# A section that ends without its own drain of GpSimd: bias and softmax over 571 MB on one core

## The chip, the cores and the metric

One core of one Trainium2 chip. The metric is the device time of one execution in microseconds (us); a kernel is run several times and the median is given. A profile is one execution, so its span can differ by a few us from the median.

## The reference

```python
B, H, S = (2, 8, 2112)          # logits: B x H x S x S, float32; rel_bias: H x 33
rel_clipped = np.clip(pos[:, None] - pos[None, :], -16, 16) + 16
logits = logits + rel_bias[:, rel_clipped][None]
logits = logits - logits.max(axis=-1, keepdims=True)
exp = np.exp(logits)
return exp / exp.sum(axis=-1, keepdims=True)
```

Each row of 2112 logits gets a bias that depends on the distance from the diagonal, and a softmax. 285 MB are read and 285 MB written.

## The kernel before

The 128 partitions hold 6 rows each, 50,688 bytes, in one of four buffers; 44 such loads and stores make the whole. GpSimd issues the loads (but half of the first one), SyncE issues the stores. VectorE adds the bias (a strip made once), ScalarE takes the exponential with the row sum, VectorE inverts and multiplies. The four engines' parts are written by hand, with semaphores, inside one critical section. These are the parts that matter here:

```python
    section = ctx.enter_context(tc.tile_critical(name="rows"))        # L74
    ...
    def take(eng, sem, v):
        eng.wait_ge(sem, v).then_inc(sem, -v)                           # L88
    def load(eng, u, start):
        eng.dma_start(out=L[u][:], in_=rows(logits, start)).then_inc(loaded[u], 16)   # L91
    def reload(eng, u, start):
        take(eng, stored[u], 16)          # the buffer's store has landed
        load(eng, u, start)
    ...
    def sync_part(eng):
        ...                               # 44 stores (L97), then:
        for n in range(BUFS):
            take(eng, stored[n], 32 if n < 2 else 16)   # all of them have landed

    def gpsimd_part(eng):
        row_load(eng, 1, loaded[0])       # half of the first buffer
        ...                               # loads 1 to 3
        passes(eng, BUFS, lambda u, start, loads: reload(eng, u, start))   # 40 loads
        eng.drain()                       # L246, the part's own drain
    ...
    with _tile.TileContext(nc) as tc:     # L291: the program's start and end
```

At the end of a critical section each engine that took part runs a drain (an instruction that ends when all of the engine's earlier work is done) and signals SyncE. The program then ends with two more rounds in which all engines meet, with further drains. (A NOP only waits for a signal and gives one.)

The softmax here doesn't subtract the row's maximum and nothing guards it: scores larger than these inputs give would overflow.

Of the kernel before, what the change touches and what calls it, by code (L numbers as in the profile page):

```python
# [14 lines left out]
def kernel(  # L15
# [55 lines left out]
            tensor=t.tensor, offset=t.offset + start * S, ap=[[T * S, P], [1, run]]  # L71
        )

    section = ctx.enter_context(tc.tile_critical(name="rows"))  # L74
    loaded = [nc.alloc_semaphore(f"loaded{u}") for u in range(BUFS)]
    stored = [nc.alloc_semaphore(f"stored{u}") for u in range(BUFS)]
    table = nc.alloc_semaphore("table")
# [218 lines left out]
```

## Time and profile before

| | |
|---|---|
| time, median of the first three runs | 1329.33 us (1326.05 to 1329.79) |
| span in the profile | 1324.4 us |
| VectorE, ScalarE, GpSimd busy | 71%, 40%, 3% |
| DMA | 431 GB/s over the span, busy in every slice |
| last store landed, to the last instruction's end | 1323.276 to 1324.411 us: 1.135 us |

The table is read from the bottom: the stream of transfers fills the time until SyncE sees its last store land, and what the ending adds after that is 1.1 us.

### The profile page before, as it was taken

To read this page: it belongs to the slowest core of one execution; us is meant where nothing else is said; L and a number is where in the kernel's file an instruction comes from. 1 tells how busy PE (TensorE), PEld (TensorE's weight loads), DVE (VectorE), ACT (ScalarE), POOL (GpSimd) and SP (SyncE) were. 2 spreads that over 40 slices of the span, in tenths; PEclk is the share of its full clock that TensorE was granted. 3 is DMA by queue.
4 is the path that set the end of the run, shared out by engine and by line. 5 is a ranking of instruction groups with operands and counts; after the bars stand their busy time and mean duration, and the time that the engine had idled before them with its cause. 6 is when DMAs were issued, how large, how long until landed. Compare 5 with 4: busy or idle time off the path is not lost. (4 is left out here: it accounts for less than half of the span.)

```text
span 1324.4 us, 2004 instructions
## 1 busy us (share of the span) xinstructions
DVE 941.6 (71%) x451; ACT 524.9 (40%) x530; POOL 39.8 (3%) x50
## 2 busy tenths in 40 slices
DVE  4989776677777767667777767667777776766891
ACT  0645533333444443333344443333344443333360
POOL 0000000000000000000000000000000000000000
DMA  9999999999999999999999999999999999999998
GB/s 392 438 424 437 436 433 429 439 435 427 436 435 435 430 438 435 430 433 436 435 429 439 435 429 435 438 433 430 438 435 429 435 438 433 430 438 435 432 431 371
DMA packets 13762, 570.99 MB, mean 431 GB/s; under 512 B 1600, under 2 KB 1600, under 8 KB 1600
## 3 DMA queue, kind: packets, MB, share of 16 engines
q1 hardware_dynamic: 7024, 288.72, 50.4%
q0 software_dynamic: 6592, 282.23, 49.3%
q10 hardware_dynamic: 144, 0.02, 0.0%
q14 instruction: 2, 0.02, 0.0%
HBM read 285.49 MB, written 285.47 MB: 431 GB/s over the span
## 5 line engine op out<-in xcount | busy, mean ns | idle before, releaser
L125 ACT ACTIVATE L<-L 128x2112 f32<-128x2112 f32 x264 | 515.2, 1952 | 766.7 <-ACTq L88 766.7
L118 DVE TENSOR_TENSOR L<-L,F 128x6336 f32<-128x6336 f32 x88 | 590.7, 6754 | 230.5 <-DMA L<-in_logits_dram 229.7
L139 DVE TENSOR_SCALAR L<-L,tot 128x2112 f32<-128x2112 f32 x264 | 332.5, 1315 | 13.2 <-DVEq L88 0.8
L135 DVE RECIPROCAL tot<-tot 128x3 f32<-128x3 f32 x88 | 15.2, 172 | 96.9 <-DVEq L88 96.9
L91 POOL DMA_DIRECT2D L<-in_logits_dram x43 | 38.4, 894 | 1202.6 <-POOLq L88 1202.6
L125 ACT ACTIVATION_READ_ACCUMULATOR L<-L 128x1 f32 x264 | 49.2, 186 | 0.0
L179 DVE TENSOR_SCALAR L<-L,rbP 128x71 f32<-128x71 f32 x1 | 0.3, 258 | 12.1 <-DVEq L88 12.1
L187 DVE TENSOR_TENSOR F<-L,rbP 128x2343 f32<-128x2343 f32 x1 | 2.6, 2600 | 0.1
L188 DVE TENSOR_TENSOR F<-F,L 128x2343 f32<-128x2343 f32 x1 | 2.6, 2598 | 0.1
L252 ACT ACT_TABLE_LOAD x1 | 1.3, 1283 | 2.9 <-issue 2.9
L174 DVE TENSOR_SCALAR L<-L 128x71 int32<-128x71 int32 x1 | 0.2, 198 | 3.1 <-DVEq L88 3.1
L208 POOL DMA_DIRECT2D L<-in_logits_dram x1 | 0.9, 882 | 1.1 <-PEq L291 1.1
L177 DVE TENSOR_SCALAR L<-L 128x71 f32<-128x71 f32 x3 | 0.6, 197 | 0.4
L182 DVE SCALAR_TENSOR_TENSOR L<-L,rbP 128x71 f32<-128x71 f32 x1 | 0.3, 294 | 0.2 <-DVEq L88 0.2
L175 DVE TENSOR_TENSOR L<-L 128x71 f32<-128x71 int32 x1 | 0.2, 234 | 0.1
L180 DVE COPY F<-rbP 128x16 f32<-128x16 f32 x1 | 0.2, 176 | 0.1
L186 DVE COPY F<-rbP 128x16 f32<-128x16 f32 x1 | 0.2, 175 | 0.1
L234 POOL IOTA L<- 128x71 int32 x1 | 0.2, 207 | 0.1
L237 POOL IOTA L<- 128x71 int32 x1 | 0.2, 208 | 0.0
L252 ACT ACTIVATE one<-const-float32-0.0 128x1 f32<-128x1 f32 x1 | 0.2, 203 | 0.0
L280 POOL MEMSET const-float32-0.0<- 128x1 f32 x1 | 0.1, 99 | 0.4 <-issue 0.4
L280 POOL MEMSET const-bfloat16-1.0<- 128x1 bf16 x1 | 0.1, 103 | 0.0
(2 smaller groups left out, 0.2 us busy)
## 6 DMA issues: line engine op xcount, KB each, us to landing
L<-in_logits_dram POOLq DMA_DIRECT2D x43, 6336.0 KB, 39.4
out_dram<-L SPq DMA_DIRECT2D x42, 6336.0 KB, 55.0
out_dram<-L SPq DMA_DIRECT2D x4, 3168.0 KB, 45.9
L<-in_logits_dram SPq DMA_DIRECT2D x1, 3168.0 KB, 15.3
L<-in_logits_dram POOLq DMA_DIRECT2D x1, 3168.0 KB, 17.8
rbP<-in_rel_bias_dram ACTq DMA_DIRECT2D x2, 8.2 KB
```

The lines of the kernel that those rows point to most:

```text
L91: eng.dma_start(out=L[u][:], in_=rows(logits, start)).then_inc(loaded[u], 16)
L118: eng.tensor_tensor(out=x3, in0=x3, in1=F3, op=ALU.add).then_inc(added, 1)
L125: e = eng.activation(out=x, in_=x, func=EXP, accum_out=tot[u][:, i : i + 1])
L135: eng.reciprocal(out=t, in_=t).then_inc(inverted, 1)
L139: e = eng.tensor_scalar_mul(out=x, in0=x, scalar1=tot[u][:, i : i + 1])
L177: step(eng.tensor_scalar(out=m, in0=qm, scalar1=0.0, scalar2=None, op0=op))
L179: step(eng.tensor_scalar(out=rest, in0=lt, scalar1=low, scalar2=None, op0=ALU.mult))
L182: eng.scalar_tensor_tensor(out=rest, in0=gt, scalar=high, in1=rest, op0=ALU.mult, op1=ALU.add)
L187: step(eng.tensor_tensor(out=blocks, in0=wide(eq), in1=rev, op=ALU.mult))
L188: step(eng.tensor_tensor(out=blocks, in0=blocks, in1=wide(rest), op=ALU.add))
L208: eng.dma_start(out=bass.AP(tensor=x.tensor, offset=x.offset + r0 * S, ap=[[list(x.ap[0])[0], P], [2 * S, R // 2], [1, S]],), in_=bass.AP( ...
L252: eng.activation(out=one, in_=nc.const_aps.tensor(0.0, [P, 1], FP32), func=EXP)
```

## The change

The GpSimd part drains its queue itself (L246), so the drain that the section adds for GpSimd looks like a second one for the same thing. The section has an option to leave it out; the intent is to save it.

```diff
-    section = ctx.enter_context(tc.tile_critical(name="rows"))
+    section = ctx.enter_context(tc.tile_critical(name="rows", no_gpsimd_drain=True))
```

## The prediction

> **What bounds the kernel now.** I began with the page's busy shares and its 40 slices. VectorE is the busiest engine, at 71% of the span, and ScalarE has 40%, so no compute engine is the limit. The DMA row and the totals are different:
>
> ```profile
> DMA  9999999999999999999999999999999999999998
> GB/s 392 438 424 437 436 433 429 439 435 427 436 435 435 430 438 435 430 433 436 435 429 439 435 429 435 438 433 430 438 435 429 435 438 433 430 438 435 432 431 371
> ...
> HBM read 285.49 MB, written 285.47 MB: 431 GB/s over the span
> ```
>
> In 39 of 40 slices the 16 DMA engines are busy for 90% or more, and 285.49 + 285.47 = 570.96 MB at 431 GB/s makes 1325 us, which is the span of 1324.4 us. The kernel is a stream of one read and one write of everything, and the stream has no gap. Only its last slice falls to 371 GB/s. That is the end, and it is the only place that this change can touch, so I cut it by stages (us, then busy time of VectorE, ScalarE and GpSimd with instruction counts, clock, DMA share, GB/s):
>
> ```profile
> 1250.00:1275.00 25.00, 21.13 (x10) 11.89 (x12) 0.00 (x0) 1.00 0.99 426
> 1275.00:1299.00 24.00, 21.27 (x11) 11.90 (x12) 0.00 (x0) 1.00 1.01 437
> 1299.00:1325.00 26.00, 0.00 (x0) 0.00 (x0) 0.00 (x0) 1.00 0.80 347
> ```
>
> After 1299 us no engine computes; only the last 6336 KB store is on its way (one DMA in the view of issues from 1298 us on, 24.4 us from issue to landing, issued at 1298.86). So the end of the kernel is: last multiply, store, the store's landing, then the exit of the section and of the program.
>
> The chain of waits that the page prints stops at the last VectorE multiply and so does not show this part. I took it from the view of single lines. The line of the section (L74), the line where the launch opens and closes the tile context (L291), and the GpSimd part's own drain (L246):
>
> ```profile
> L246 POOLq DRAIN  x1: 31907/31907/31907, 1243.5 to 1243.5; - x1
> ```
>
> ```profile
> L74 SPq EVENT_SEMAPHORE  x3: 17/17/28, 1323.3 to 1323.5; - x3
> L74 SPq NOP  x2: 13/13/13, 0.9 to 1323.6; - x2
> L74 ACTq DRAIN  x1: 13/13/13, 1323.4 to 1323.4; - x1
> L74 POOLq DRAIN  x1: 47/47/47, 1323.4 to 1323.4; - x1
> L74 DVEq DRAIN  x1: 17/17/17, 1323.4 to 1323.4; - x1
> L74 SPq DRAIN  x1: 7/7/7, 1323.4 to 1323.4; - x1
> ```
>
> ```profile
> L291 POOLq EVENT_SEMAPHORE  x4: 17/17/17, 1323.8 to 1324.3; - x4
> L291 POOLq DRAIN  x3: 34/34/78, 1323.5 to 1324.2; - x3
> ```
>
> Columns: line, queue, operation, count, duration in ns (shortest, median, longest), first and last start in us. The reader is to see three things. The explicit drain is the long one: 31.907 us from 1243.5 to 1275.4, all of it beside the loads, the arithmetic and the stores of the last four buffers, and it is over 48 us before the end. The section's own GpSimd drain, which the change removes, is 47 ns at 1323.4. And three more GpSimd drains follow in the program's end, which the change does not mention.
>
> **What the Trainium skill says.** "PSUM — Partial Sum Buffer", section "Engine vs sequencer instructions", has it that a "drain waits for the engine to go fully idle". The trace agrees where GpSimd has something open: the explicit drain starts just after the last load is issued (1243.38) and ends 1.8 us after that load has landed (30.2 us later, 1273.6). With nothing open the next one takes 47 ns. "VectorE: DVE Perf Modes", section "The DRAIN you can't avoid", gives drains of a program's preamble and postamble as a constant of some 12 ns on all five engines. Here the exit drains of SyncE, ScalarE and VectorE take 7 to 17 ns, in agreement, but GpSimd's take 34 to 78 ns. "Perfetto Trace Analysis", section "Per-engine timelines", says that a sequencer instruction is shown from the moment its semaphores are met, and that the wait before it and the travel of its signal after it are not shown. So the 47 ns are execution alone, and I must work out the signal's travel from the gaps. "DMA: Bandwidth & Descriptors", section "Where 436 GB/s comes from", puts the ceiling at 435.2 GB/s; the steady slices here move 427 to 439, so it agrees, and nothing in the stream itself is to be won.
>
> **The change, part by part.** It removes one instruction that runs once: GpSimd's drain at the section's exit. It adds and moves no work in the loops; each of the 44 iterations' loads, adds, exponentials, multiplies and stores stays.
>
> What that drain costs depends on who waits for it. The trace's records give the exit in ns, with the semaphore of each:
> - SyncE's wait for the last store is met at 1323.276 us; at 1323.336 it signals all engines that the section ends.
> - The four drains: ScalarE 1323.374 for 13 ns, GpSimd 1323.377 for 47 (done 1323.424), VectorE 1323.381 for 17 (done 1323.398), SyncE 1323.407 for 7.
> - SyncE then takes their signals one instruction after the other: VectorE's at 1323.481, its own and ScalarE's at 1323.540, GpSimd's by a NOP at 1323.611; the next step is at 1323.686.
>
> VectorE's signal takes at most 83 ns from the end of its drain to SyncE's wait (1323.481 less 1323.398). If GpSimd's takes as long, an estimate from that number, it is there at 1323.507, while SyncE reaches the instruction that asks for it only at 1323.611. So the 47 ns have about 104 ns of slack: shortening them to nothing is worth 0.
>
> A gain is possible only if SyncE's list gets shorter. Its steps there are 59, 71, 75 and 63 ns apart (the starts 1323.481, .540, .611, .686, .749). With GpSimd's signal gone there are three waits left, and they may fit one instruction fewer: one step, some 0.07 us. On GpSimd's side the program's first closing drain (34 ns at 1323.486) would come earlier, but what GpSimd waits for next is the gather of the other engines, met at 1323.781 after SyncE's drain at 1323.749, so 0.26 us of slack there and again nothing gained.
>
> Sum: 0 from the drain, 0 to 0.07 us from SyncE's list, at most 0.14 us if two steps go. My figure is 0.05 us, or 0.004% of 1329 us. An upper bound needs no guess: from the landing of the last store (1323.276) to the last record (1324.41) there are 1.13 us. Had the change removed the whole exit, it would be 0.09%. Two per cent is 26.6 us.
>
> **The rivals.**
> - *The drain is dear, because a GpSimd drain is.* The 31.9 us of L246 are the right size for 2.4%, and anyone who reads only the durations expects about 1298 us. Against it: it is another instruction, which the change keeps, its time lies beside the DMA stream, and nothing waits for it before the exit. I give this 1%.
> - *Another wait takes its place.* The exit may get a plain semaphore instruction on GpSimd in the drain's stead (GpSimd's take 17 ns here), and the program's closing drain then meets whatever was left open. Since the explicit drain left nothing open, that is 34 ns as now. The time would be the same within 0.1 us. This and the shorter list can't be told apart by time.
> - *GpSimd no longer waits for the section's end and runs ahead* to the program's closing drain at 1275.4 us. It would wait there for the other engines instead, 48 us long, and the end would not move, because SyncE's wait for the last store holds the gather.
> - *Slower.* A different place of GpSimd's later instructions could cost a fetch, but it would have to hit inside the load loop to delay a transfer, and VectorE's and SyncE's programs do not change at all in their loops. I see at most 1 or 2 us, hence no verdict.
> - *Scatter looks like an effect.* The three runs are 1326.05, 1329.33 and 1329.79, the profiled run 1326.06: two clusters 3.5 us apart, seventy times the gain I expect. A median may fall into either of them, so a difference of 3 us between before and after is no effect of the change.
>
> **Range and chances.** The mean of the three runs is 1328.4, their median 1329.33. With an effect of 0.05 us the time after is a draw from the same two clusters, more likely from the upper (two of three timed runs): I say 1328.8 us, and give the range the clusters with some 1 to 2 us on either side for another day and chip: 1325.2 to 1331.5. Faster by over 2% needs 26.6 us from an exit that lasts 1.13 us: 0.01. Slower by over 2%: 0.01. Within 2%: 0.98.
>
> **What would show it right or wrong.** In the changed kernel's profile the section's line should have no GpSimd drain, or a semaphore instruction in its place; L246 should still be a drain of about 32 us that ends near 1275; the stretch from the landing of the last store to the last record should last 1.0 to 1.15 us instead of 1.13; the DMA totals, 431 GB/s and the counts of all compute groups should not change. The prediction is wrong if the explicit drain of L246 vanishes or moves past the last store, if a later GpSimd drain grows to microseconds, or if the DMA row shows a gap that it lacks now.

## The result, and the profile after

The changed kernel took 1327.17 us (median of 4 runs, 1325.86 to 1327.87), the kernel before 1327.69 us in the four runs that were timed with it (1326.01 to 1329.79). The ratio is 0.9994 with a 95% interval from 0.9974 to 1.0015: the same.

The program's instructions on VectorE, ScalarE, SyncE and the tensor engine are the same as before, one for one. On GpSimd there is one difference. This is the view of the section's line in the changed kernel (line, queue, operation, count, shortest, median and longest duration in ns, first and last start in us):

```profile
L74 SPq EVENT_SEMAPHORE  x3: 17/17/28, 1324.6 to 1324.8; - x3
L74 SPq NOP  x2: 13/13/13, 0.9 to 1324.9; - x2
L74 ACTq DRAIN  x1: 13/13/13, 1324.6 to 1324.6; - x1
L74 POOLq NOP  x1: 17/17/17, 1324.6 to 1324.6; - x1
L74 DVEq DRAIN  x1: 17/17/17, 1324.6 to 1324.6; - x1
L74 SPq DRAIN  x1: 7/7/7, 1324.7 to 1324.7; - x1
```

GpSimd's drain of 47 ns has become a NOP of 17 ns that waits for the same signal and gives the same one. SyncE's list is as long as it was. The closing drains and the part's own drain, in the changed kernel:

```profile
L291 POOLq EVENT_SEMAPHORE  x4: 17/17/17, 1325.0 to 1325.6; - x4
L291 POOLq DRAIN  x3: 34/47/77, 1324.7 to 1325.4; - x3
```

```profile
L246 POOLq DRAIN  x1: 32247/32247/32247, 1244.4 to 1244.4; - x1
```

The three closing drains took 34, 78 and 34 ns before and take 47, 77 and 34 ns now: the first drain after the wait costs 47 ns whichever one it is, and the 13 ns that the removed one had more than a second drain have gone over to the next. The own drain is still 32 us long and still ends (at 1276.7 us) some 49 us before the end.

The trace's records in ns show that nothing was gained. From the instruction that sees the last store land to the one with which SyncE takes GpSimd's signal there are 335 ns in both kernels (1323.276 to 1323.611 before, 1324.541 to 1324.876 after), and from there to the end of the last instruction 800 and 799 ns. The span of this profile is 1.3 us longer, because the last store landed 1.3 us later; that is scatter of the stream, as the next section shows.

### The profile page after: what moved, and what is told of

Same layout as the page of the kernel before. It is cut to its first block, busy times and chain, and to the rows that moved or that the text cites. A ratio compares the mean times of both kernels' runs of the same rounds, so it can differ in the third digit from the quotient of the medians.

```text
span 1325.7 us, 2004 instructions
## 1 busy us (share of the span) xinstructions
DVE 941.8 (71%) x451; ACT 524.9 (40%) x530; POOL 35.1 (3%) x50
## 3 DMA queue, kind: packets, MB, share of 16 engines
q0 software_dynamic: 6592, 282.23, 49.3%
## 5 line engine op out<-in xcount | busy, mean ns | idle before, releaser
L91 POOL DMA_DIRECT2D L<-in_logits_dram x43 | 33.8, 786 | 1208.2 <-POOLq L88 1208.2
L208 POOL DMA_DIRECT2D L<-in_logits_dram x1 | 0.9, 880 | 1.1 <-PEq L291 1.1
```

The source lines that it names most:

```text
L208: eng.dma_start(out=bass.AP(tensor=x.tensor, offset=x.offset + r0 * S, ap=[[list(x.ap[0])[0], P], [2 * S, R // 2], [1, S]],), in_=bass.AP( ...
```

## The experiments

Line numbers shift by some lines in edited kernels: the section stays L74, the program's end is L290 to L308.

### The pair again, and the kernel before against itself

No edit in either: `a1_after_again` is the changed kernel, `a2_before_again` the kernel before, both with five rounds against the kernel before, on one chip.

> The changed kernel once more, with more rounds. My theory (the removed drain lay beside SyncE's own list of signals): ratio to the kernel before 1.000, within 0.15% either way; from the landing of the last store to the last record 1.13 us again. Rival (the drain was on the path and the first four runs were too few to show it): at most 0.05 us, so 0.004%, which these rounds can't see either; only the records' order at the end can, and there the rival expects SyncE's NOP for GpSimd's signal less than 335 ns after the landing.

> The kernel before against itself, unchanged: what scatter alone makes of the ratio. Expected 1.000 with an interval of about 0.1 to 0.2% to either side, and single runs between 1325.8 and 1330 us. If this pair differs as much as the changed kernel does from before, the small difference of the medians seen so far (1327.17 against 1327.69) is scatter.

The changed kernel took 1326.22 us (1326.06 to 1326.76), ratio 0.9990 [0.9978, 1.0003]. The kernel before, under a second name, took 1326.82 us (1325.20 to 1330.66), ratio to itself 0.9995 [0.9980, 1.0010]. So two identical kernels differ by nearly as much as the changed one and the old one did at first (0.9994), and single runs of one kernel lie 5 us apart. In both the ending is what it was: 335 ns from landing to the NOP and 1.134 us to the end. No difference is shown in time, and none in the length of the ending.

### Take the own drain away as well, and take only the own drain away

```diff
# b1_no_drain_at_all: the changed kernel without L246
# b2_section_drain_only: the kernel before without L246
-        eng.drain()
```

> The changed kernel with GpSimd's own 32 us drain taken away too, so that neither is left. My theory (32 us wholly beside the stream of transfers): same time, ratio 1.000 within 0.2%; GpSimd then waits some 80 us for the section's end, and its first drain in the program's end takes 34 to 80 ns because nothing is open by then. Rival (the 32 us drain holds something up, and is the drain that should have been removed): up to 2.4% faster, about 1297 us. Second rival (a drain takes time for every transfer since the last drain, so the closing one grows): a closing drain of 1 us or more.

> The kernel before without the GpSimd part's own drain, so that the section's drain is the only one ahead of the program's end. My theory: the section's drain starts about 0.1 us after the last store has landed, finds nothing open, and takes 40 to 60 ns as now; time the same within 0.2%. Rival (the own drain is what makes the section's drain cheap): the section's drain takes microseconds, up to 32 us, and the time grows by as much less about 0.1 us of slack.

Here my theory fell, and what came true was the second rival of the first run and the rival of the second. The section's drain in the kernel without the own one, and the closing drains (L290) in the kernel without either:

```profile
L74 POOLq DRAIN  x1: 3652/3652/3652, 1323.3 to 1323.3; - x1
```

```profile
L290 POOLq DRAIN  x3: 40/78/3652, 1323.4 to 1327.4; - x3
```

GpSimd's last load had landed 50 us earlier, and still the first drain took 3652 ns, in both kernels the same. It lies on the path: from the last landing to the end there are 4.58 us with the section's drain alone and 4.51 us with neither, against 1.13 us. The times follow: 1330.05 us (1329.35 to 1330.72) without any, ratio 1.0020 [1.0005, 1.0034]; 1329.70 us with the section's drain alone, with one run at 1343.66 us that pulls the ratio to 1.0050 [1.0011, 1.0090]. So the own drain does not hold anything up, as I had said; but it is not idle either: it does 3.6 us of something that has to be done, at a time when that costs nothing.

### A hundred drains on the path

```diff
# c2_hundred_late_drains, from the changed kernel (the allocation of the semaphore is left out)
 sync_part:      take(eng, stored[n], 32 if n < 2 else 16)
+        eng.sem_inc(ended, 1)
 gpsimd_part:    eng.drain()
+        take(eng, ended, 1)
+        for _ in range(100):
+            eng.drain()
```

> The changed kernel with 100 GpSimd drains that start only when SyncE has seen the last store land, so that they lie on the path to the end and have nothing to wait for. Theory (a drain with nothing open costs its own 34 to 78 ns and a gap to the next instruction of about 30 ns, where it is on the path): 6 to 11 us more, 0.5 to 0.8%. Rival (drains are free when nothing is open): under 1 us more. Second rival (repeated drains are dearer): over 15 us.

```profile
L251 POOLq DRAIN  x100: 34/34/173, 1326.4 to 1332.9; - x100
```

From 1326.4 to 1332.9 us there are 100 drains, on average 0.066 us from one start to the next (61 ns in most steps), of which 34 ns are the drain. The ending grew from 1.13 to 7.64 us, by 6.51 us, within the 6 to 11 us expected; the time was 1333.57 us against 1328.31 us, ratio 1.0030 [0.9997, 1.0064], an interval that holds 1, so that the time by itself shows no difference. A drain that has nothing to do is cheap even on the path: 65 ns each.

### The change where GpSimd's transfer is the last one

```diff
# d1_gp_store_section_drain (from before), d2_gp_store_no_drain (from the changed kernel):
# GpSimd issues the last store when SyncE says so, and has no drain of its own
# (SyncE's part and the allocation of the two semaphores are left out)
-        eng.drain()
+        take(eng, last, 1)
+        eng.dma_start(
+            out=rows(out, (N - 1) * R), in_=L[BUFS - 1][:]
+        ).then_inc(gone, 16)
```

> The last store is issued by GpSimd instead of SyncE and the own drain is taken out, so that the section's drain follows a transfer of GpSimd's own queue that has only just landed. In the kernel before the own drain ended 1.8 us after its last transfer had landed. My theory: the section's drain starts some 0.1 us after the landing is seen, and now takes up to 1.8 us, here for once on the path; time 0 to 2 us above before. Rival (what it took was not the queue, and a drain behind a landed transfer is 47 ns): no change at the end.

> As the kernel with the last store on GpSimd, but the section without its drain: the change, in the one place where the drain has something to wait for. My theory: GpSimd's first drain in the program's end takes over what the section's drain took (within 0.1 us), and SyncE's list is passed earlier but the gather of all engines is not, so the end moves by less than 0.3 us against the other kernel. Rival (leaving the drain out saves what it took): up to 1.8 us shorter from landing to the last record.

The section's line with its drain, then the program's end without it:

```profile
L74 POOLq DRAIN  x1: 3734/3734/3734, 1331.1 to 1331.1; - x1
```

```profile
L299 POOLq DRAIN  x3: 40/78/3734, 1323.2 to 1327.3; - x3
```

The size was again not what I expected (up to 1.8 us), but the take-over was: what the section's drain is spared, the next drain takes, to the nanosecond. From the signal of SyncE that ends the section to the last instruction there are 4.60 us with the section's drain and 4.54 us without it. So the change gains 0.065 us here, as it does between the two kernels above without an own drain (4.579 and 4.514 us), and not the 3.7 us of the drain. The times (1332.46 and 1330.22 us, ratios 1.0023 [0.9990, 1.0056] and 1.0013 [0.9979, 1.0048]) can't resolve that.

These two kernels also gave the clue to the size. They issue 45 transfers from GpSimd instead of 44, and the drain is 3734 - 3652 = 82 ns longer; and 3652 is 44 times 83.

### What the 3.65 us are made of

```diff
# e1_drain_ahead_of_20, e2_drain_ahead_of_4 (n = 20 or 4), from the kernel before
-        passes(eng, BUFS, lambda u, start, loads: reload(eng, u, start))
-        eng.drain()
+        passes(eng, BUFS, lambda u, start, loads: reload(eng, u, start), N - n)
+        eng.drain()
+        passes(eng, N - n, lambda u, start, loads: reload(eng, u, start))
```

```diff
# e3_loads_cut_by_partitions: no own drain, each load in two of 64 partitions
-        eng.dma_start(out=L[u][:], in_=rows(logits, start)).then_inc(loaded[u], 16)
+        src = rows(logits, start)
+        for p0 in (0, P // 2):
+            half = bass.AP(tensor=src.tensor, offset=src.offset + p0 * T * S,
+                           ap=[[T * S, P // 2], [1, RS]])
+            eng.dma_start(out=L[u][p0 : p0 + P // 2], in_=half).then_inc(loaded[u], 16)
# e4_loads_cut_by_rows: no own drain, each load in two of 3 rows on all partitions
+        for r0 in (0, R // 2):
+            eng.dma_start(out=L[u][:, r0 * S : (r0 + R // 2) * S],
+                          in_=rows(logits, start + r0, RS // 2)).then_inc(loaded[u], 16)
```

(In the last two the first load is cut likewise, and the counts waited for are doubled.)

> The kernel before with GpSimd's own drain moved from behind its last load to ahead of its last 20, so that the section's drain has 20 of GpSimd's transfers behind it, all landed long ago. With all 44 behind it the section's drain took 3652 ns, with 45 3734 ns. New theory (a drain walks through every transfer issued since the last drain, landed or not): 34 + 20 x 82 ns = 1.68 us. Rival (a fixed cost of a first drain, with transfers of whatever number): 3.65 us again. Old theory (nothing open, nothing to pay): 47 ns. Ahead of the twenty loads the moved drain itself should take some 30 us and then 1 to 2 us after the landing, and cost the stream little.

> The same with the own drain ahead of the last 4 loads only. Walk through the transfers: 34 + 4 x 82 ns = 0.36 us for the section's drain. Fixed cost: 3.65 us. Nothing open: 47 ns.

> The kernel before without the own drain, and each of GpSimd's 44 loads cut into two of 64 partitions: 88 transfers, the same bytes, and hardly more DMA packets (80 instead of 144 for each of the halves, if the record's 144 are 128 rows and 16 semaphore writes). The section's drain, by the number of transfers: 34 + 88 x 82 ns = 7.3 us. By packets (0.55 ns each): about 4.0 us. By bytes, or a fixed cost: 3.65 us.

> The same, but each load cut into two of half the length on all 128 partitions: 88 transfers with twice the packets and the same bytes. The section's drain, by the number of transfers: 7.3 us. By packets: 7.3 us too. By bytes or a fixed cost: 3.65 us. With the cut by partitions beside it, transfers, packets and bytes are told apart.

The section's drain in the four, in this order:

```profile
L74 POOLq DRAIN  x1: 1687/1687/1687, 1324.0 to 1324.0; - x1
```

```profile
L74 POOLq DRAIN  x1: 381/381/381, 1327.6 to 1327.6; - x1
```

```profile
L74 POOLq DRAIN  x1: 7252/7252/7252, 1707.8 to 1707.8; - x1
```

```profile
L74 POOLq DRAIN  x1: 7251/7251/7251, 1393.1 to 1393.1; - x1
```

| transfers of GpSimd since its last drain | their packets | their MB | the drain, ns | 54 + 81.8 x transfers |
|---|---|---|---|---|
| 4 | not counted | 26 | 381 | 381 |
| 20 | not counted | 130 | 1687 | 1690 |
| 44 | 6592 | 282 | 3652 | 3653 |
| 45 | 6736 | 289 | 3734 | 3735 |
| 88, cut by partitions | 7296 | 282 | 7252 | 7252 |
| 88, cut by rows | 13184 | 282 | 7251 | 7252 |

The packets and MB are the software queue's in each profile (for 4 and 20, the size of a load, 6.49 MB, times the number). The slope comes from the first and the last row: (7252 - 381) / 84 = 81.8 ns. The two cuts have the same bytes as the 44 loads and packets in the ratio of 1 to 1.8, and the same drain; so it is neither bytes nor packets but the number of transfers issued since the last drain, all of which had landed here. The fixed cost and the old theory are out. (The line holds from 4 transfers on; with none, the closing drains took 34 to 78 ns and not 54.)

The moved drains themselves took 40.3 and 42.0 us, where I had expected some 30 for the first. With 24 and 40 transfers behind them they ended 1.51 and 2.15 us after the last packet of their loads; the own drain of the kernel before, with 44, ended 2.32 us after it. So what an early drain still takes after the last packet grows with the number of transfers too.

The kernels with 4 and with 44 transfers also give the slack that I had estimated at 104 ns (by how much GpSimd's signal was there before SyncE asked for it). With 4 transfers behind it the drain is 381 - 47 = 334 ns longer than in the kernel before, and SyncE takes its signal 508 ns after the landing instead of 335, 173 ns later: 161 ns had been slack. With 44 behind it (`b2_section_drain_only`), 3605 ns longer and 3444 ns later: 161 ns again.

The times, one run each beside a run of the kernel before of 1325.92 us: 1328.51 and 1330.75 us for the moved drain, inside the scatter or close to it. Cutting the loads made the stream slower, 1717.7 us by partitions and 1403.1 us by rows, with 333 and 407 GB/s over the span.

### A drain behind every load

```diff
# c1_drain_in_loop, from the changed kernel
-        passes(eng, BUFS, lambda u, start, loads: reload(eng, u, start))
+        def reload_and_drain(u, start, loads):
+            reload(eng, u, start)
+            eng.drain()
+        passes(eng, BUFS, reload_and_drain)
```

> The changed kernel with a GpSimd drain behind each of the 40 loads of its loop, so that a drain stands ahead of the next load's issue. Each should last from the issue to some 1.8 us after the load has landed, 30 to 40 us, 1200 us or more in all. My theory (what counts is whether the DMA engines run out of work): the next load is issued up to 2.5 us after the last one has landed, and in that gap the store in flight takes the whole rate, so the stream hardly thins: 0 to 2% slower, 1327 to 1354 us. Rival 1 (each drain's gap after landing is lost): 40 x 1.8 = 72 us, 5.4% slower, about 1400 us. Rival 2 (each drain's time is paid): the time nearly doubles.

It took 1384.28 us (1382.28 to 1388.14), ratio 1.0414 [1.0373, 1.0455]: between my 0 to 2% and the first rival's 5.4%, so both missed. The 40 drains, and two stretches of the loop (us, busy time of VectorE, ScalarE and GpSimd with counts, clock, DMA share, GB/s):

```profile
L246 POOLq DRAIN  x40: 23507/32062/38729, 82.5 to 1315.7; - x40
```

```profile
657.00:694.00 37.00, 21.25 (x10) 11.90 (x12) 0.53 (x1) 1.00 0.99 412
694.00:719.00 25.00, 21.24 (x10) 11.90 (x12) 0.53 (x1) 1.00 0.91 395
```

The 40 drains last 32 us each at the median, 1.23 ms together, and cost 55 us (0.0414 x 1328), 1.4 us each. So neither the drain's length nor nothing is paid. In the first stretch the DMA engines stay busy; in the second, whose store had landed before the gap, they idle for a tenth of it. My figure for the gap was 1.8 us after a landing, taken from the own drain of the kernel before, which has 44 transfers to go through. With one transfer a drain ended 0.41 us (median) after the load's last packet, where the own drain of the kernel before ended 2.32 us after it. That is why 72 us was too much as the drains' part; but 40 x 0.41 = 16 us are not the 55 us either. The packets' times in the two profiles say more: the 16 DMA engines were busy for 1321 of 1324 us before and for 1353 of 1384 us here. So of the 60 us between these spans some 29 are idle engines, and some 31 are the same packets taking longer. Why they do, and how the rest divides into drain, issue and an emptier queue, is not shown.

## Why the prediction was right

- **The bound, and the size of the ending.** Right: 431 GB/s before and 1324.411 - 1323.276 = 1.135 us of ending, 1.134 us after. The time was 1327.17 us in a range of 1325.2 to 1331.5; the point, 1328.8, leaned on the upper of two clusters that more runs dissolved into one band from 1325 to 1330 us, with one run at 1335.41; that it came within 1.6 us is scatter, not insight. In the reading of the slices, the third one has 424 GB/s, under the 427 given for the steady ones, and the upper ones (to 439) lie over the cited ceiling of 435.2; the mean of 431 does not.
- **Who waits for the drain.** Right, and the step that mattered: SyncE asks for GpSimd's signal last. The slack was 161 ns, measured, where I had estimated 104, because I took the signal's travel from VectorE's (83 ns at most; where SyncE waited for GpSimd's drain, it took the signal 26 ns after the drain's end).
- **The gain of 0 to 0.07 us from a shorter list of SyncE.** Wrong in its small part: the list was not shortened, because GpSimd gives its signal with a NOP. The second rival, "Another wait takes its place", is what happened, and its effect on the time was 0.
- **What the closing drain finds.** The outcome was right (47 ns instead of 34), its reason was not complete. I wrote "With nothing open the next one takes 47 ns". It takes 47 ns because no transfer was issued since the drain before it. With 44 issued, all landed 50 us ago, it takes 3652 ns. The own drain had done that work by 1275.4 us.
- **The drain of 31.9 us beside the stream.** Right, and half the story. Taking it away saves nothing and adds 3.4 us to the ending (4.51 against 1.13 us), because its share of 3.65 us falls to whichever drain comes first.

So the change is worth nothing in time for two reasons. What it removes had 161 ns of slack, and was 47 ns only because the own drain stood before it. And without the own drain the next drain takes over what the removed one took, so that only 0.065 us are gained. Of the pair, the own drain is the one to keep. No version that I ran beats both kernels.

## What to carry to other kernels

Before a drain or a wait is removed as double, look at which of the two does the work and where: on this kernel the early drain pays for all of GpSimd's transfers beside the stream, and the late one pays nothing because of it. Price an ending from the trace's records between the last landing and the last instruction; if that is 0.1% of the time, no shortening of it can show in runs that scatter like these. An instruction's duration is its cost only where somebody waits for its end: 32 us of drain cost nothing at the end of the part, and 1.4 us each in the loop, with all that they changed there.

## What the Trainium skill lacked or had wrong

- "PSUM — Partial Sum Buffer", section "Engine vs sequencer instructions", says that a drain waits until the engine is idle. That is not all it does on GpSimd: with everything landed it took 54 ns and 82 ns for each transfer issued since the last drain (381 ns for 4, 3652 ns for 44, 7252 ns for 88), whatever their bytes and packets. No page that I read has this.
- "VectorE: DVE Perf Modes", section "The DRAIN you can't avoid", has some 12 ns for drains in a program's start and end on all engines. GpSimd's took 34 to 78 ns with nothing behind them (100 in a row: 34 ns at the median, and mostly a step of 61 ns), and microseconds with transfers behind them.
